# A two-layer streaming encoder on one core: who computes the low halves of the weights beside the recurrence

## The chip, the core and the metric

The kernel runs on one core of a Trainium2 chip. The metric is the device time of one execution in microseconds (us). A core has five engines with a queue of their own, each in program order: TensorE (PE, matmul; PEld is its weight load), VectorE (DVE), ScalarE (ACT), GpSimd (POOL) and SyncE (SP, which here issues all transfers).

## The reference

The reference runs two layers over 1,024 prompt frames and 64 frames of a running stream, each of width 1,024: a layer of RWKV-7 time mixing, a layer of sliding-window attention, and a SwiGLU FFN after each. The first layer matters here.

```python
xr = x + xx * mu[0]            # xx: the previous frame less this one; likewise xk, xv, xw, xa, xg
r = xr @ w_rkv[0]; k = xk @ w_rkv[1]; v = xv @ w_rkv[2]
...
def step(s, inp):              # one frame; s is a 64x64 matrix per head, 16 heads
    r_t, w_t, k_t, v_t, a_t, b_t = inp
    sa = jnp.einsum('bhvk,bhk->bhv', s, a_t)
    s = s * w_t[:, :, None, :] + sa[..., None] * b_t[:, :, None, :] + v_t[..., None] * k_t[:, :, None, :]
    return s, jnp.einsum('bhvk,bhk->bhv', s, r_t)
s_fin, y = lax.scan(step, s0, seq_in)
out = ((groupnorm(y) + bonus) * g) @ w_o
x = x + out
x = x + swiglu(rmsnorm(x, norm_ffn[l]), ffn_w_in[l], ffn_w_out[l])
```

## The kernel before, in words

**Two halves.** The frames are cut into half A (512 prompt frames, chunks 0 to 7 of 64 frames) and half B (512 prompt frames and the 64 of the running stream, chunks 8 to 16). Activations lie with features on the partitions and frames along the free axis.

**Dense products in three matmuls.** `Dense` cuts each operand into a high half (rounded to `fp32r`) and a low half (the remainder), and `mm` adds three products: high by high (L604), low activation by high weight (L605), high activation by low weight (L606). A weight tile of 128x1024 comes in two pieces of 128x512. `piece` loads one (`wr`, L563, by SP), rounds it on ScalarE (`wh`, L564) and subtracts (`wl`, L565). The subtraction runs on GpSimd for every third piece and on VectorE for the other two. There are three buffers for `wr` and six each for `wh` and `wl`. Of half B a dense tile is two groups of 290 columns, so 24 matmuls into one PSUM bank `dp` for each group.

**The recurrence in chunks.** For each chunk `prep` loads r, k, a, s from DRAM and forms scaled operands (GpSimd takes the products of L151, L176, L177), `inverse32` solves a triangular system with a long row of small VectorE steps (L268 and L272 in turn), `chain` runs five groups of matmuls from the old state to the new one (L447 and L448 write the new state, `r_M`), and `post` normalises the chunk's output: L489 on VectorE, L490 and L491 on GpSimd, a transpose on TensorE (L113, into `p_ry`), L496 and L497 on VectorE, and a store to `s_z` (L498). The next chunk's chain needs this chunk's state.

**What runs beside what.** `recur_free(range(8), ...)` issues chunks 0 to 7. Behind it in the code, at a lower priority on TensorE, stand the projections v, r and k of half B (`rkv("B", ...)`, 24 weight tiles, so 48 pieces), their mixes (L850, L851, L597) and the small decay, rate and gate products of half B. A scheduler with a timeline of its own merges all of this into one fixed order for each engine, and each engine then runs its queue in that order. Half A's next step, `mixed_in` and `mix_out` (L1059, L596, L1071), needs `s_z` of all of chunks 0 to 7. Chunks 8 to 16 run later, beside half A's FFN.

Of the kernel before, what the change touches and what calls it, by code (L numbers as in the profile page):

```python
# [12 lines left out]
ALU = mybir.AluOpType  # L13
# [8 lines left out]
def bc(ap, n):  # L22

    return ap.unsqueeze(len(ap.shape)).broadcast_to(list(ap.shape) + [n])
# [7 lines left out]
class Two:  # L32


    def __init__(self, tc):
        self.tc, self.pe = tc, 0
# [48 lines left out]
class Rwkv:  # L85
# [331 lines left out]

    def chain(self, ch, d, M):

        nc = self.nc  # L420
        V, S, G = nc.vector, nc.scalar, nc.gpsimd

        sv = self.t([128, 16, 64], "sv")
        nc.sync.dma_start(sv[64:128].rearrange("p a b -> p (a b)"), self.scr["vt"][ch * 64:ch * 64 + 64, :])
        svh = sv.rearrange("p (j par) v -> p j par v", par=2)
        V.tensor_copy(svh[0:64, :, 0, :], M[0:64])
        S.copy(svh[0:64, :, 1, :], M[64:128])
        E = lambda x: x.rearrange("p (a b) -> p a b", a=8)
        X, W = d["X"], self.W
        heads = [(i, i // 2, slice(64 * (i % 2), 64 * (i % 2) + 64)) for i in range(16)]  # L430
        U0p = E(self.pc())
        for i, j, h in heads:
            self.mm(U0p[h, j, :], lhsT=X[:, 8 * (i % 2) + j, 0:64], rhs=sv[:, i, :], start=True, stop=True)
        U0 = self.tmp()
        S.copy(U0, U0p)
        yield
        Up = E(self.pc())
        for i, j, h in heads:
            self.mm(Up[h, j, :], lhsT=W[h, j, :], rhs=U0[h, j, :], start=True, stop=True)
        V.tensor_copy(svh[0:64, :, 0, :], Up[0:64])  # L440
        S.copy(svh[0:64, :, 1, :], Up[64:128])
        yield
        Sp = E(self.pc())
        for i, j, h in heads:
            self.mm(Sp[h, j, :], lhsT=d["BT"][:, i, :], rhs=sv[:, i, :], start=True, stop=True)
        Mn = d["M"] = self.t([128, 8, 64], "M", 2)
        V.tensor_tensor(out=Mn, in0=Sp, in1=M, op=ALU.add)  # L447
        V.tensor_tensor(out=Mn, in0=Mn, in1=bc(d["PC"], 64), op=ALU.mult)  # L448
        yield


        Y = E(self.p([128, 512], "ry", 1))
        out = lambda j, par: Y[64 * (j % 2):64 * (j % 2) + 64, j // 2 * 2 + par, :]

        def seen(par):
            h = slice(64 * par, 64 * par + 64)
            return [self.mm(out(j, par), lhsT=d["AR"][h, j, 1, :], rhs=M[h, j, :], start=par == 0 and j < 2, stop=False) for j in range(8)]
        even = seen(0)
        by = G.memset(self.t([1, 1], "by", 2), 0.0)
        yield  # L460

        odd = seen(1)
        for i, first in ((by, even[-1]), (odd[0], by)):
            info = mybir.DependencyInfo(mybir.DependencyClass.Sync, mybir.DependencyReason.DATA)
            self.tc.add_manual_dep(i.ins, first.ins.name, info, reason="rows")
        for q in range(0, 8, 2):
            for j, par in ((q, 0), (q + 1, 0), (q, 1), (q + 1, 1)):
                self.mm(out(j, par), lhsT=X[:, 8 * par + j, 64:128], rhs=sv[:, 2 * j + par, :], start=False, stop=q == 6 and par == 1)
        d["Y"] = Y
        yield  # L470
# [51 lines left out]
class Dense:  # L522


    def __init__(self, tc, sb, ps, c):
        self.tc, self.nc, self.sb, self.ps, self.c = tc, tc.nc, sb, ps, c
        self.n = self.turn = 0
        self.more = self.esb = self.pump = None
        self.mixed = []
        self.spare, self.early = deque("x" * RING), deque()  # L530

    def t(self, shape, tag, bufs, dt=F32, sb=None):
# [24 lines left out]
    def piece(self, src, rows=128, raw=None):  # L557
        nc = self.nc
        n = src.shape[1]
        hi, lo = self.t([128, 512], "wh", 6, F32R), self.t([128, 512], "wl", 6, F32R)  # L560
        self.turn += 1
        x, h, l = (raw or self.raw)()[:rows, :n], hi[:rows, :n], lo[:rows, :n]
        nc.sync.dma_start(x, src)  # L563
        nc.scalar.copy(h, x)  # L564
        (nc.gpsimd if self.turn % 3 == 0 else nc.vector).tensor_tensor(out=l, in0=x, in1=h, op=ALU.subtract)  # L565
        return h, l

    @staticmethod
# [177 lines left out]
def tile_stream_step(ctx: ExitStack, tc: tile.TileContext, I, O):  # L746
    nc = tc.nc
# [8 lines left out]
    dn = Dense(tc, sb, ps, c)  # L756
# [42 lines left out]
    def put(name, half, j, stg):  # L799

        c0 = halves[half][2]
        dst = scr[name][c0:c0 + 8, :, j * 64:j * 64 + 64].rearrange("c p t -> p c t")
        nc.sync.dma_start(dst, stg[:, 0:512].rearrange("p (c t) -> p c t", t=64))
        if half == "B":
            nc.sync.dma_start(scr[name][16, :, j * 64:j * 64 + 64], stg[:, SOFF:SOFF + 64])
# [175 lines left out]
    def rkv(half, name, xs, ws=()):  # L981

        T, groups = mixed[half]
        tok0 = halves[half][2] * 64

        def tokens(j, stg):

            p = dn.bank()
            for b in range(4):
                nc.tensor.transpose(p[:, b * 128:b * 128 + 128], stg[:, b * 128:b * 128 + 128], c["id"])  # L990
            vt = dn.st()
            copy_out[half](vt[:, :512], p)
            nc.sync.dma_start(scr["vt"][tok0:tok0 + 512, j * 128:j * 128 + 128].rearrange("(b t) f -> t b f", t=128),
                              vt[:, :512].rearrange("t (b f) -> t b f", f=128))
            if half == "B":
                p = dn.bank()
                nc.tensor.transpose(p[:64, :128], stg[:, SOFF:SOFF + 64], c["id"])
                vt = dn.st()
                copy_out[half](vt[:64, :128], p[:64, :128])
                nc.sync.dma_start(scr["vt"][1024:1088, j * 128:j * 128 + 128], vt[:64, :128])  # L1000

        old = None
        w, early = I["rkv"]["rkv".index(name)], [dn.st() for _ in ws]
        if ws:
            dn.first(ws, xs, groups, lambda j, o, n, p: S.copy(early[j][:, o:o + n], p))
        for j in range(8):
            if j < len(early):
                stg = early[j]
            else:
                stg = dn.st()  # L1010
                dn.full(w[j], xs, groups, lambda o, n, p: copy_out[half](stg[:, o:o + n], p))
            put(name, half, j, stg)
            if name == "v":
                if old:
                    tokens(*old)
                old = (j, stg)
            if j == 7:
                dn.free(*xs)
            yield
        if old:  # L1020
            tokens(*old)
# [3 lines left out]
    def all(gen):  # L1025
        for _ in gen:
            pass
# [138 lines left out]
    def prio(p):  # L1166
        tc.cur_priority = int(p * 1000000)
# [37 lines left out]
    def recur_free(chunks, M, base, low):  # L1205

        def prep(i):
            all(rw.prep(chunks[i], ds[i], wide=True))

        def prep2(i):  # L1210
            rw.inverse32(ds[i])
            rw.turned(ds[i])
        ds = [{} for _ in chunks]
        rw.two.at(base, base)
        prep(0)
        prep2(0)
        for i, ch in enumerate(chunks):
            late = 0.001 * i
            if i + 1 < len(chunks):
                rw.two.at(base + 0.301 + late, low + 0.301 + late)  # L1220
                prep(i + 1)
            rw.two.at(base + late, base + late)
            all(rw.chain(ch, ds[i], M))
            M = ds[i]["M"]
            rw.two.at(base + late, low + late)
            all(rw.post(ch, ds[i]))
            if i + 1 < len(chunks):
                rw.two.at(base + 0.1 + late, base + 0.1 + late)
                prep2(i + 1)
        return M  # L1230
# [78 lines left out]
        step(old, fill)  # L1309

    M = recur_free(range(8), M, 1, LOW)
    prio(2)
    r, k = (mixes("B", hB, n) for n in "rk")
    stage = several(4, chain(deB, raB, gaB))
# [2 lines left out]
    go(rkv("B", "r", xs["Br"]), chain(stage, several(2, take(RING - 8, k))))  # L1317
    all(k)
    all(rkv("B", "k", xs["Bk"]))
    pump = dn.pump = Pump(tc)  # L1320

    def saved(M):
# [79 lines left out]
class Attention:  # L1402
# [170 lines left out]
    def out(self, xs, x, hv, norm):  # L1573
        nc, dn, I = self.nc, self.dn, self.I
        T, groups, _ = hv
        for j in range(8):
            dn.full(I["wo"][j], xs, groups,
                    lambda o_, n, p: nc.vector.scalar_tensor_tensor(
                        out=x[j][:, o_:o_ + n], in0=p, scalar=self.vec["b_o"][:, j:j + 1], in1=x[j][:, o_:o_ + n],
                        op0=ALU.add, op1=ALU.add))  # L1580
            norm.add(x[j][:, :T])
            if j == 7:
                dn.free(*xs)
            yield
# [107 lines left out]
```

## Time and profile before

| | |
|---|---|
| median of three runs | 3019.65 us (3019.26 to 3027.69) |
| the profiled execution: its own time | 3027.17 us |
| its span, first to last instruction | 3025.4 us, 53,491 instructions |
| busy time by engine | PE 2837.6, DVE 1835.6, ACT 1344.4, POOL 916.4 us |
| mean granted TensorE clock | 0.965 of 2.4 GHz |

The profiled execution lies 7.52 us above the median, near the slowest of the three runs. "Busy" counts the time in which an engine had an instruction under way; a VectorE instruction that is held by something else after it was issued counts as busy.

### The profile page before, as it was taken

To read this page: it belongs to the slowest core of one execution; us is meant where nothing else is said; L and a number is where in the kernel's file an instruction comes from. 1 tells how busy PE (TensorE), PEld (TensorE's weight loads), DVE (VectorE), ACT (ScalarE), POOL (GpSimd) and SP (SyncE) were. 2 spreads that over 40 slices of the span, in tenths; PEclk is the share of its full clock that TensorE was granted. 3 is DMA by queue.
4 is the path that set the end of the run, shared out by engine and by line. 5 is a ranking of instruction groups with operands and counts; after the bars stand their busy time and mean duration, and the time that the engine had idled before them with its cause. 6 is when DMAs were issued, how large, how long until landed. Compare 5 with 4: busy or idle time off the path is not lost. (4 is left out here: it accounts for less than half of the span.)

```text
span 3025.4 us, 53491 instructions
## 1 busy us (share of the span) xinstructions
PE 2837.6 (94%) x20802; PEld 2443.9 (81%) x20802; DVE 1835.6 (61%) x3630; ACT 1344.4 (44%) x2485; POOL 916.4 (30%) x795
## 2 busy tenths in 40 slices
PE   6998888887999999999999999999999999999998
PEld 5777777875677777787789999887777888999997
DVE  8887789976778677467553333665644345533334
ACT  6767665543444444244653222344554233322222
POOL 5554124422333333224212222243111222222221
PEclk9999878998999999999999999999999999999999
DMA  4645352345233323432212222222222332322222
GB/s 146 165 123 147 111 155 81 107 113 149 67 92 106 105 84 93 128 118 84 62 50 70 84 84 81 77 84 80 61 69 77 94 94 70 112 83 81 83 84 70
DMA packets 262053, 289.22 MB, mean 96 GB/s; under 512 B 125028, under 2 KB 143972, under 8 KB 261800
## 3 DMA queue, kind: packets, MB, share of 16 engines
q1 hardware_dynamic: 261800, 285.81, 32.0%
q8 instruction: 163, 2.67, 0.4%
q14 instruction: 90, 0.74, 0.1%
HBM read 243.18 MB, written 41.16 MB: 94 GB/s over the span
## 5 line engine op out<-in xcount | busy, mean ns | idle before, releaser
L604 PE MATMUL dp<-xh,wh 128*128 128x288 f32 (+2 forms) x3480 | 1189.6, 343 | 41.6 <-ACT xh L596 15.1
L605 PE MATMUL dp<-xl,wh 128*128 128x288 f32 (+2 forms) x3480 | 1167.8, 336 | 7.5 <-DVE xl L597 5.3
L606 PE MATMUL dp<-xh,wl 128*128 128x288 f32 (+2 forms) x3480 | 1163.1, 334 | 0.0
L564 ACT CAST wh<-wr 128x512 fp32r<-128x512 f32 x730 | 446.9, 619 | 812.8 <-PE dp L605 624.8
L604 PEld LDWEIGHTS dp<-xh,wh 128*128 128x128 f32 x3480 | 664.9, 191 | 124.9 <-ACT xh L596 18.0
L605 PEld LDWEIGHTS dp<-xl,wh 128*128 128x128 f32 x3480 | 665.7, 191 | 69.5 <-DVE xl L597 9.0
L606 PEld LDWEIGHTS dp<-xh,wl 128*128 128x128 f32 x3480 | 665.9, 191 | 56.8 <-issue 2.8
L565 POOL TENSOR_TENSOR wl<-wr,wh 128x512 fp32r<-128x512 f32 x243 | 336.5, 1385 | 1036.2 <-ACT wh L564 944.9
L565 DVE TENSOR_TENSOR wl<-wr,wh 128x512 fp32r<-128x512 f32 x487 | 377.6, 778 | 422.6 <-ACT wh L564 416.4
L604 PE MATMUL dp<-mh,wh 128*128 128x288 f32 (+1 forms) x808 | 254.4, 315 | 4.5 <-DVE hx L1135 2.8
L606 PE MATMUL dp<-mh,wl 128*128 128x288 f32 (+1 forms) x808 | 253.8, 314 | 0.0
L605 PE MATMUL dp<-ml,wh 128*128 128x288 f32 (+1 forms) x808 | 253.7, 314 | 0.0
L1135 DVE TENSOR_TENSOR a_xB<-dp,a_xB 128x288 f32<-128x288 f32 x352 | 158.1, 456 | 85.2 <-PE dp L606 84.8
L1118 POOL TENSOR_TENSOR xl<-st,xh 128x288 fp32r<-128x288 f32 (+1 forms) x102 | 100.6, 986 | 332.3 <-ACT xh L1117 320.0
L1116 DVE TENSOR_TENSOR st<-st,dp 128x288 f32<-128x288 f32 (+1 forms) x132 | 70.1, 531 | 203.7 <-PE dp L606 203.2
L604 PEld LDWEIGHTS dp<-mh,wh 128*128 128x128 f32 x808 | 152.3, 189 | 15.1 <-DVE hx L1135 3.9
L606 PEld LDWEIGHTS dp<-mh,wl 128*128 128x128 f32 x808 | 152.3, 188 | 8.6 <-issue 2.4
L605 PEld LDWEIGHTS dp<-ml,wh 128*128 128x128 f32 x808 | 152.4, 189 | 6.9 <-issue 1.1
L1135 DVE TENSOR_TENSOR hx<-dp,hx 128x512 f32<-128x512 f32 x176 | 119.5, 685 | 42.1 <-PE dp L606 41.2
L1117 ACT CAST xh<-st 128x288 fp32r<-128x288 f32 (+1 forms) x102 | 50.2, 492 | 127.5 <-DVE st L1116 126.4
L1114 ACT ACTIVATE st<-dp 128x288 f32<-128x288 f32 (+1 forms) x132 | 62.2, 471 | 87.5 <-PE dp L606 87.0
L597 POOL TENSOR_TENSOR xl<-st,xh 128x512 fp32r<-128x512 f32 (+2 forms) x37 | 64.7, 1758 | 68.5 <-ACT xh L596 68.5
(378 smaller groups left out, 3851.9 us busy)
## 6 DMA issues: line engine op xcount, KB each, us to landing
wr<-in_ffn_in SPq DMA_DIRECT2D x352, 256.0 KB
wr<-in_ffn_out SPq DMA_DIRECT2D x176, 256.0 KB
wr<-in_rkv SPq DMA_DIRECT2D x90, 256.0 KB
wr<-in_rwo SPq DMA_DIRECT2D x32, 256.0 KB
wr<-in_wq SPq DMA_DIRECT2D x32, 256.0 KB
wr<-in_wo SPq DMA_DIRECT2D x32, 256.0 KB
r_r_s<-s_s SPq DMA_DIRECT2D x17, 256.0 KB
r_sv<-s_vt SPq DMA_DIRECT2D x17, 256.0 KB
```

Source lines behind the costliest of these rows:

```text
L564: nc.scalar.copy(h, x)
L565: (nc.gpsimd if self.turn % 3 == 0 else nc.vector).tensor_tensor(out=l, in0=x, in1=h, op=ALU.subtract)
L597: (eng or self.nc.vector).tensor_tensor(out=lo, in0=x, in1=hi, op=ALU.subtract)
L604: self.nc.tensor.matmul(ps, lhsT=wh, rhs=xh, start=i == 0, stop=False)
L605: self.nc.tensor.matmul(ps, lhsT=wh, rhs=xl, start=False, stop=False)
L606: self.nc.tensor.matmul(ps, lhsT=wl, rhs=xh, start=False, stop=i == last)
L1114: S.activation(t[o], p, AF.Silu)
L1116: V.tensor_tensor(out=t[o], in0=t[o], in1=p, op=ALU.mult)
L1117: S.copy(a.hi[:, q], t[o])
L1118: G.tensor_tensor(out=a.lo[:, q], in0=t[o], in1=a.hi[:, q], op=ALU.subtract)
L1135: V.tensor_tensor(out=self.x[m][:, q], in0=p, in1=self.x[m][:, q], op=ALU.add)
```

## The change: what it does

`Dense` gets a field `share`, which takes the place of the constant 3. It is 3 everywhere but in the code that issues the projections of half B, where it is 1: there every piece's subtraction goes to GpSimd. Of these 48 pieces 16 were on GpSimd before; 32 move from VectorE's queue to GpSimd's. Nothing else is written differently, but the scheduler builds every queue anew.

```diff
@@ class Dense, __init__
         self.mixed = []
+        self.share = 3
         self.spare, self.early = deque("x" * RING), deque()
@@ piece
         nc.scalar.copy(h, x)
-        (nc.gpsimd if self.turn % 3 == 0 else nc.vector).tensor_tensor(out=l, in0=x, in1=h, op=ALU.subtract)
+        (nc.gpsimd if self.turn % self.share == 0 else nc.vector).tensor_tensor(out=l, in0=x, in1=h, op=ALU.subtract)
@@ tile_stream_step
     M = recur_free(range(8), M, 1, LOW)
+
+    dn.share = 1
     prio(2)
     r, k = (mixes("B", hB, n) for n in "rk")
     stage = several(4, chain(deB, raB, gaB))
     go(rkv("B", "v", xs["Bv"]), chain(wait(3), take(8 - 3, stage)))
     all(r)
     go(rkv("B", "r", xs["Br"]), chain(stage, several(2, take(RING - 8, k))))
     all(k)
     all(rkv("B", "k", xs["Bk"]))
+    dn.share = 3
     pump = dn.pump = Pump(tc)
```

Line numbers of the changed kernel are one higher from L530 on, three from L1313 and four from L1323. The queues differ in three places that the prediction speaks of.

**GpSimd in the middle of the recurrence.** The rows are those of the prep of chunk 4 (`r_rt_3763`, `r_rkr_3776`) with the post steps of chunks 1 and 2 beside it (`r_sm_3266`, `r_yc_3269`; `r_sm_3600`, `r_yc_3603`); `wl` are the pieces. Before:

```order
L490 TENSOR_TENSOR r_sm_3266<-r_sm_3266,power 128x8
L565 TENSOR_TENSOR wl_6300<-wr_6301,wh_6299 128x512
L491 TENSOR_TENSOR r_yc_3269<-r_yc_3269,r_sm_3266 128x512
L479 TENSOR_TENSOR r_vf_3493<-r_vf_3493,vecs 128x512
L151 TENSOR_TENSOR r_rt_3763<-r_r_k_3756,vecs 128x8x64
L459 MEMSET r_by_3569 1x1
L156 MEMSET r_rt_3767 128x8
L480 TENSOR_TENSOR r_vf_3159<-r_vf_3159,r_g_3595 128x512
L481 TENSOR_TENSOR r_g_3595<-r_g_3595,vecs 128x512
L176 TENSOR_TENSOR r_rkr_3776<-r_rkr_3776,r_r_r_3755 128x512
L177 TENSOR_TENSOR r_rkr_3776<-r_rkr_3776,vecs 128x512
L565 TENSOR_TENSOR wl_6489<-wr_6490,wh_6488 128x512
```

Of the change, from L481 of `r_g_3595` up to the same piece `wl_6489`:

```order
L481 TENSOR_TENSOR r_g_3595<-r_g_3595,vecs 128x512
L566 TENSOR_TENSOR wl_6294<-wr_6295,wh_6293 128x512
L566 TENSOR_TENSOR wl_6300<-wr_6301,wh_6299 128x512
L151 TENSOR_TENSOR r_rt_3763<-r_r_k_3756,vecs 128x8x64
L156 MEMSET r_rt_3767 128x8
L566 TENSOR_TENSOR wl_6415<-wr_6416,wh_6414 128x512
L176 TENSOR_TENSOR r_rkr_3776<-r_rkr_3776,r_r_r_3755 128x512
L177 TENSOR_TENSOR r_rkr_3776<-r_rkr_3776,vecs 128x512
L566 TENSOR_TENSOR wl_6421<-wr_6422,wh_6420 128x512
L490 TENSOR_TENSOR r_sm_3600<-r_sm_3600,power 128x8
L491 TENSOR_TENSOR r_yc_3603<-r_yc_3603,r_sm_3600 128x512
L566 TENSOR_TENSOR wl_6489<-wr_6490,wh_6488 128x512
```

Between `wl_6300` and `wl_6489` nine steps of the recurrence stood in a row; now two more pieces stand between them, two steps apart, and L151, with which the prep of a chunk begins, stands right behind two pieces.

**The end of chunk 7.** On GpSimd, L490 and L491 of the last chunk of half A (`r_sm_5193`, `r_yc_5196`) and what stands behind them; `wl_7589`, `wl_7636` and `wl_7745` belong to half A's next product, `r_rt_7470` to the prep of chunk 8. Before:

```order
L565 TENSOR_TENSOR wl_7589<-wr_7590,wh_7588 128x512
L481 TENSOR_TENSOR r_g_5188<-r_g_5188,vecs 128x512
L490 TENSOR_TENSOR r_sm_5193<-r_sm_5193,power 128x8
L565 TENSOR_TENSOR wl_7636<-wr_7637,wh_7635 128x512
L491 TENSOR_TENSOR r_yc_5196<-r_yc_5196,r_sm_5193 128x512
L151 TENSOR_TENSOR r_rt_7470<-r_r_k_7463,vecs 128x8x64
L156 MEMSET r_rt_7474 128x8
L151 TENSOR_TENSOR r_rt_7887<-r_r_k_7880,vecs 128x8x64
L176 TENSOR_TENSOR r_rkr_7483<-r_rkr_7483,r_r_r_7462 128x512
```

Of the change:

```order
L490 TENSOR_TENSOR r_sm_5193<-r_sm_5193,power 128x8
L491 TENSOR_TENSOR r_yc_5196<-r_yc_5196,r_sm_5193 128x512
L566 TENSOR_TENSOR wl_7589<-wr_7590,wh_7588 128x512
L566 TENSOR_TENSOR wl_7636<-wr_7637,wh_7635 128x512
L566 TENSOR_TENSOR wl_7745<-wr_7746,wh_7744 128x512
L151 TENSOR_TENSOR r_rt_7470<-r_r_k_7463,vecs 128x8x64
L156 MEMSET r_rt_7474 128x8
L698 TENSOR_TENSOR lo_7586<-lo_7586,st_7626 128x512
L151 TENSOR_TENSOR r_rt_7887<-r_r_k_7880,vecs 128x8x64
L176 TENSOR_TENSOR r_rkr_7483<-r_rkr_7483,r_r_r_7462 128x512
```

The piece between L490 and L491 has gone behind them, and the prep of chunk 8 (L151) stands behind three pieces more. On TensorE, the transpose of chunk 7's output (`p_ry_5153`), the last tiles of B's k projection (`dp_7365`, `dp_7406`, `dp_7432`) and the first of half A's next product (`dp_7560`). Before:

```order
L606 MATMUL dp_7432<-xh_6913,wl_7401 128x290
L604 MATMUL dp_7432<-xh_6920,wh_7400 128x290
L605 MATMUL dp_7432<-xl_6921,wh_7400 128x290
L606 MATMUL dp_7432<-xh_6920,wl_7401 128x290
L113 MATMUL p_ry_5153<-c_id,r_yc_5196 128x128 x4
L604 MATMUL dp_7560<-xh_7494,wh_7548 128x512
L605 MATMUL dp_7560<-xl_7495,wh_7548 128x512
```

Of the change:

```order
L605 MATMUL dp_7365<-xh_6913,wh_7333 128x290
L606 MATMUL dp_7365<-xl_6914,wh_7333 128x290
L113 MATMUL p_ry_5153<-c_id,r_yc_5196 128x128 x4
L607 MATMUL dp_7365<-xh_6913,wl_7334 128x290
L605 MATMUL dp_7365<-xh_6920,wh_7333 128x290
L606 MATMUL dp_7365<-xl_6921,wh_7333 128x290
L607 MATMUL dp_7365<-xh_6920,wl_7334 128x290
L605 MATMUL dp_7406<-xh_6402,wh_7394 128x290
```

Before, all dense matmuls of half B stand ahead of the transpose; now 53 stand behind it. Counted in the order, of the 1,657 dense matmuls (L604 to L606) that stand ahead of `dp_7560`, 1,498 stood ahead of chunk 6's state product (`p_rc` from `r_BT`) before and 1,425 stand there now; up to the same product of chunk 7 another 123 before and 101 now; from there to the transpose 35 before and 78 now.

**The hand-over on SyncE.** The store of chunk 7's output (`s_z`) and what stands around it: `r_r_k` are loads for the preps of chunks 8 and 9, `hx` the loads of half A's next product. Before:

```order
L148 DMA r_r_k_7463<-s_k 128x512
L148 DMA r_r_k_7880<-s_k 128x512
L498 DMA s_z<-r_vf_4829 128x512
L478 DMA r_g_8669<-s_g 128x512
L1059 DMA hx_7492<-s_z 128x8x64
L1059 DMA hx_7499<-s_z 128x8x64
L1059 DMA hx_7506<-s_z 128x8x64
```

Of the change:

```order
L804 DMA s_k<-st_7326 128x8x64
L806 DMA s_k<-st_7326 128x64
L498 DMA s_z<-r_vf_4829 128x512
L564 DMA wr_7692<-in_rwo 128x512
L478 DMA r_g_8669<-s_g 128x512
L1060 DMA hx_7492<-s_z 128x8x64
L1060 DMA hx_7499<-s_z 128x8x64
```

The two loads of `r_r_k`, which wait for the last store of `s_k`, stood ahead of the store of `s_z` and now stand behind the loads of `hx`; L169 of chunk 8, which needs the first of them, has gone behind L497 of chunk 7 on VectorE in the same way.

## Rows read from the trace of the kernel before

**Rows 1.** The page: busy time of two engines; shares of the last chain.

```profile
PE 2837.6 (94%) x20802; PEld 2443.9 (81%) x20802; DVE 1835.6 (61%) x3630; ACT 1344.4 (44%) x2485; POOL 916.4 (30%) x795
PE 34%; DVE 2%; issue 0%; ACT 0%; DMA 0%; SPq 0%; DVEq 0%; ACTq 0%
```

**Rows 2.** Windows: stretch and length (us), busy time by engine (instructions), clock, DMA.

```profile
230.00:390.00 160.00, 140.22 (x1146) 120.96 (x1145) 123.05 (x298) 107.11 (x176) 54.15 (x46) 0.88 0.47 134
390.00:645.00 255.00, 220.68 (x2293) 197.94 (x2292) 233.28 (x622) 149.02 (x235) 92.13 (x71) 0.87 0.39 107
645.00:671.00 26.00, 26.00 (x364) 24.83 (x363) 14.22 (x29) 9.64 (x19) 7.56 (x9) 1.00 0.50 136
671.00:687.00 16.00, 1.53 (x7) 0.97 (x5) 6.28 (x10) 3.95 (x7) 9.29 (x8) 0.61 0.62 160
```

**Rows 3.** Groups by line, 390 to 645 us: busy, mean ns; idle before, releaser.

```profile
L565 DVE TENSOR_TENSOR wl<-wr,wh 128x512 fp32r<-128x512 f32 x21 | 17.3, 825 | 0.0
...
L210 DVE TENSOR_TENSOR r_G<-p_rp,c_mask 128x512 f32<-128x512 f32 x20 | 13.7, 683 | 3.0 <-PE p_rp L109 2.9
...
L248 DVE STREAM_TRANSPOSE r_f<-r_f 128x1024 f32<-128x1024 f32 x5 | 6.2, 1245 | 12.3 <-ACT r_f L243 12.3
```

**Rows 4.** The same view of GpSimd, 390 to 645 us.

```profile
L565 POOL TENSOR_TENSOR wl<-wr,wh 128x512 fp32r<-128x512 f32 x11 | 14.8, 1344 | 50.0 <-ACT wh L564 47.7 <-issue 2.3
```

**Rows 5.** One line's instructions, whole run: duration ns min/median/max.

```profile
L565 DVE TENSOR_TENSOR wl<-wr,wh x487: 647/692/1954, 40.4 to 2988.8; 128x512 fp32r<-128x512 f32 x163
...
L565 POOL TENSOR_TENSOR wl<-wr,wh x243: 1257/1294/3645, 41.0 to 2987.3; 128x512 fp32r<-128x512 f32 x122
```

**Rows 6.** Timeline (start, duration): first and last GpSimd piece, VectorE beside them.

```profile
416.61 1.27 POOL L565 TENSOR_TENSOR wl<-wr,wh 128x512 fp32r<-128x512 f32 x1 [2.16 <-ACT wh L564]
417.87 0.69 DVE L219 TENSOR_TENSOR r_vf<-p_rp,r_vf 128x512 f32<-128x512 f32 x1 [3.10 <-PE p_rp L109]
...
644.54 1.46 POOL L565 TENSOR_TENSOR wl<-wr,wh 128x512 fp32r<-128x512 f32 x1 [10.73 <-ACT wh L564]
644.78 1.25 DVE L484 TENSOR_SCALAR r_sm<-r_sm 128x8 f32<-128x8 f32 x1
```

**Rows 7.** Two VectorE lines over the whole run: duration ns min/median/max.

```profile
L484 DVE TENSOR_SCALAR r_sm<-r_sm x17: 151/171/1252, 357.1 to 1252.9; 128x8 f32<-128x8 f32 x17
...
L497 DVE TENSOR_TENSOR r_vf<-r_g,r_vf x17: 676/691/1780, 373.5 to 1261.2; 128x512 f32<-128x512 f32 x17
```

**Rows 8.** Timeline of the end of chunk 7, several engines, in order of time.

```profile
664.20 0.27 PE L109 MATMUL p_rc<-r_sv,r_BT 128*64 128x64 f32 x1
...
666.22 0.41 PE L605 MATMUL dp<-xl,wh 128*128 128x290 f32 x1
...
666.60 0.29 PE L604 MATMUL dp<-xh,wh 128*128 128x290 f32 x1
...
667.00 0.30 PE L604 MATMUL dp<-xh,wh 128*128 128x290 f32 x1
...
672.56 1.26 POOL L565 TENSOR_TENSOR wl<-wr,wh 128x512 fp32r<-128x512 f32 x1
...
674.88 1.11 PE L113 MATMUL p_ry<-c_id,r_yc 128*128 128x128 f32 x4 [3.72 <-POOL r_yc L491]
...
676.08 0.69 DVE L496 TENSOR_TENSOR r_g<-p_ry,r_g 128x512 f32<-128x512 f32 x1 [5.20 <-issue]
...
677.69 0.69 DVE L169 SCALAR_TENSOR_TENSOR r_rkr<-r_rkr,r_r_k 128x512 f32<-128x512 f32 x1 [0.91 <-DMA r_r_k<-s_k]
...
677.73 1.55 POOL L151 TENSOR_TENSOR r_rt<-r_r_k,vecs 128x512 f32<-128x512 f32 x1 [2.91 <-DMA r_r_k<-s_k]
...
678.30 1.53 DVE L497 TENSOR_TENSOR r_vf<-r_g,r_vf 128x512 f32<-128x512 f32 x1
...
679.86 0.32 SPq L498 DMA_DIRECT2D s_z<-r_vf  x1
...
686.74 0.80 PE L604 MATMUL dp<-xh,wh 128*128 128x512 f32 x1 [10.75 <-ACT xh L596]
```

## The prediction

> **What bounds the kernel now.** I read the page first. The last chain ends almost wholly on TensorE, and VectorE is busy for 61% of the span [rows 1]; over the whole run moving 32 VectorE instructions would be worth nothing. But the change touches only the time in which half B's projections run beside chunks 0 to 7, about 230 to 671 us, so I then read windows. From 390 to 645 us VectorE is busy 233.28 of 255 us and TensorE 220.68, at a clock of 0.87 [rows 2]. The groups by line say what VectorE's idle 21.7 us are: 12.3 wait for ScalarE's copies ahead of L248, 2.9 for TensorE ahead of L210 [rows 3], another 3.1 for TensorE ahead of L219 [rows 6]. So in this stretch VectorE sets the pace of the recurrence. From 645 to 671 us it is the reverse: TensorE is busy all the time, VectorE 14.22 of 26 us. From 671 to 687 us TensorE does next to nothing [rows 2]: it waits 3.72 us for L491 and then, after chunk 7's transposes, 10.75 us for that chunk's output to go to DRAM and come back [rows 8]. Behind this TensorE is near its limit to the end, so the time of the whole kernel moves with the start of half A's next product at 686.74 us.
>
> **The change part by part.** *What leaves VectorE.* In 390 to 645 us it makes 21 pieces, 17.3 us at 825 ns [rows 3]; the other 11 of the 32 lie earlier.
>
> *What comes back as blocking.* A piece takes GpSimd 1294 ns where VectorE needs 692 [rows 5]. And VectorE does not run free beside it. In the first GpSimd piece of the stretch L219, which reads PSUM, takes its usual 0.69 us; in the last, L484 takes 1.25 us [rows 6] where its median is 171 ns [rows 7]. I went through all 11 pieces of rows 4 in this way: 10 lengthen a VectorE instruction, by 10.3 us together, 0.94 us for each of the 11. Most of those held are L268 steps, which have both inputs in SBUF; some are copies. Twenty-one more pieces cost 21 x 0.94 = 19.7 us. The net of the stretch is 19.7 - 17.3 = +2.4 us. Its bounds: nothing is held (L219), -17.3; each piece holds VectorE for its whole 1.29 us, 27.1 - 17.3 = +9.8. I take 0.94 because it is of the same instruction in the same stretch.
>
> The Trainium skill (SBUF — State Buffer, Who interferes with whom) has a rule for this: GpSimd and VectorE share one pair of SBUF ports, an instruction of VectorE with two SBUF inputs or in a two-port mode competes with a GpSimd instruction that reads SBUF, and whoever starts first keeps the pair for its whole instruction. The rows agree on who is held and who is not; if VectorE were always caught at the start, the stretch would be worth +9.8 and the sum below would be 3022.9 us.
>
> *The 11 earlier pieces.* From 230 to 390 us VectorE is busy 123.05 of 160 us [rows 2], so its idle 37 us hide a change of 0.94 - 0.825 = 0.12 us a piece. I cost them at nothing; without that cover they cost 1.3 us.
>
> *TensorE's order.* The scheduler counts VectorE relieved and puts the recurrence earlier against the dense work: 73 dense matmuls fewer ahead of chunk 6's state product. Two L604 starts with two other matmuls between are 667.00 - 666.60 = 0.40 us apart, 0.133 us for each [rows 8], so this is 9.7 us of TensorE. Where VectorE sets the pace most of it is idle time anyway; only what VectorE waits for TensorE can be won, 2.9 + 3.1 = 6.0 us [rows 3, 6]. I take half, -3.0, between 0 and -6.0.
>
> *The end of chunk 7.* From chunk 6's state product to chunk 7's TensorE is full [rows 2], and 101 dense matmuls stand there for 123: 22 x 0.133 = -2.9 us. From there to the transposes took 674.88 - 664.20 = 10.7 us, with the GpSimd piece at 672.56 between L490 and L491 [rows 8]. That piece is gone, but 78 dense matmuls stand there for 35, and with the 2.0 us of chain matmuls ahead of them (664.20 to 666.22) TensorE needs 78 x 0.133 + 2.0 = 12.4: +1.7. After the transposes L496 starts at 676.08 and L497 ends at 679.83; between them lie a wait of 0.91 us and L169, both for chunk 8, and L497 itself is held to 1.53 us by chunk 8's L151 [rows 8]. All of this is moved behind. L497 would end at 676.08 + 0.69 + 0.69 = 677.46: -2.4. The 53 dense matmuls now behind the transposes are 7.1 us and fit in the hole of 10.75 - 2.4 = 8.4 us; if the hole closes further they cost the difference. Together -2.9 + 1.7 - 2.4 = -3.6 us, between -6.0 and, if GpSimd brings L491 late, 0.
>
> *What is late next.* L151, L169 and the loads of chunk 8 start some 10 us later. Three tiles of 24 dense matmuls stand ahead of chunk 8's first matmul in both orders and cover it. `wl_7589`, `wl_7636` are late by the length of two pieces; their tiles come after `hx`, at 686.74 or a little before. Each piece needs its cast, then GpSimd; 48 pieces of 1.3 us are 62 us in more than 400, so GpSimd's throughput is no bound: in the stretch it was busy 92.13 of 255 us [rows 2] and gets 27 more.
>
> **The sum.** +2.4 - 3.0 - 3.6 = -4.2 us. Against the profiled execution's own 3027.17 us that is 3023.0; that execution stands 7.5 us above the median of the three runs, so against the median it is 3019.65 - 4.2 = **3015.5 us**.
>
> **The rivals.** *The blocking is small.* If the new pieces fall on PSUM reads, reductions and transposes as often as not, half of 0.94 us is lost for each: 9.9 - 17.3 = -7.4 in the stretch, with the other terms -14.0, 3005.6 us. For it speaks the first piece of rows 6; against it that only 1 in 11 got off free.
>
> *GpSimd's queue becomes the wait (slower).* A piece waits at the head of GpSimd's queue until ScalarE has cast it: 47.7 us for the 11 pieces [rows 4], 4.3 us each. Nothing behind it moves. Before, nine steps of the recurrence stood between two pieces; now L151 of a prep stands right behind two, and the prep's Square, norm and triangular solve hang on it. If that makes each of the stretch's five solves (L248 x5, rows 3) late by 4.3 us, it is +21.7, by half of that +10.8; in the middle +16.3, and 3015.5 + 16.3 = 3031.8 us. It decides from 13.3 us on, 2.7 us a chunk. Against it speaks that a prep runs about a chunk ahead of its use, and that a piece whose cast is done waits for nothing.
>
> *The change does nothing that counts.* If the pace of the stretch is set by the chain across engines rather than by VectorE's load, and the hole at 671 us only moves, the time stays at 3019.7 us.
>
> The Trainium skill (GPSIMD Engine Reference, Engine selection) advises against two-input elementwise work on GpSimd, at about half of VectorE's rate; 1294 against 692 ns agrees. By that alone the change would be a loss only if GpSimd were full, which it is not.
>
> **How the numbers follow.** A measurement of this kernel can tell about 0.3%, 9 us, from no change. Chances: my sum 0.45, small blocking 0.25, GpSimd's queue 0.20, nothing 0.10. Faster than 3010.6: 0.23 of the second and 0.11 of my own case, whose range is 3007 to 3025 (the stretch 7 us either way, the other terms 3); 0.34. Slower than 3028.7: 0.16 of the third and 0.02 of the first; 0.18. The rest, 0.48, lies within. The range for 8 in 10 runs from 3002, a little beyond the small blocking, to 3031, where the queue's case is half in.
>
> **What would show it.** Right: VectorE still busy some 230 of 255 us in the stretch though 21 instructions poorer, with L268's mean up; L490 and L491 of chunk 7 adjacent; L497 of that chunk about 0.69 us; dense matmuls in the hole behind the transposes; half A's next product some 4 us earlier. Wrong: L248 and L447 of each chunk earlier than before by 2 us more each time (small blocking), or L151 with long idle times behind pieces and VectorE idle ahead of the solves (the queue). What would make the prediction wrong is above all a price of blocking other than 0.94 us, which is read from 11 pieces and multiplied by 21.

## The result, and the profile after

The changed kernel takes 3039.54 us, median of five runs (3038.56 to 3045.52). Five runs of the kernel before, timed beside it, have the median 3027.69 (3019.26 to 3030.08): the three shown above lay low. The ratio is 1.0047, 95% interval 1.0035 to 1.0059, so the change costs some 14 us, 11 to 18 by the interval (ratios are turned into us here by 3027 us; the two medians lie 11.9 us apart). Predicted were -4 us.

The page of the changed kernel: busy time of the engines, and shares of the last chain.

```profile
PE 2851.9 (94%) x20802; PEld 2454.6 (81%) x20802; DVE 1826.9 (60%) x3598; ACT 1342.2 (44%) x2485; POOL 964.4 (32%) x827
PE 34%; DVE 2%; issue 0%; ACT 0%; DMA 0%; SPq 0%; DVEq 0%; ACTq 0%
```

The change did what it says: VectorE is 9 us less busy than in [rows 1], GpSimd 48 us more, and 32 instructions have gone from one to the other. The windows of the changed kernel, columns as in [rows 2]:

```profile
230.00:390.00 160.00, 138.64 (x1079) 119.96 (x1079) 108.01 (x264) 100.08 (x157) 66.10 (x54) 0.81 0.40 118
390.00:645.00 255.00, 213.66 (x2123) 188.60 (x2120) 225.06 (x575) 146.01 (x234) 117.62 (x88) 0.83 0.39 109
645.00:671.00 26.00, 25.00 (x358) 22.92 (x358) 17.95 (x62) 9.88 (x20) 9.79 (x9) 1.00 0.35 100
671.00:687.00 16.00, 16.00 (x177) 15.40 (x176) 5.33 (x10) 5.31 (x11) 5.96 (x7) 1.00 0.44 129
```

TensorE's hole from 671 to 687 us is full (its wait for half A's next product comes later now), and yet fewer of its instructions are done by 645 us (1079 + 2123 against 1146 + 2293), at a lower clock. The groups by line of the same stretch, 390 to 645 us, beside [rows 3] and [rows 4]:

```profile
L268 DVE TENSOR_TENSOR r_f<-r_f,r_f 128x48 f32<-128x48 f32 (+14 forms) x150 | 54.4, 393 | 0.2
...
L566 POOL TENSOR_TENSOR wl<-wr,wh 128x512 fp32r<-128x512 f32 x28 | 42.3, 1512 | 52.9 <-ACT wh L565 52.8
```

and that L268 group in the kernel before:

```profile
L268 DVE TENSOR_TENSOR r_f<-r_f,r_f 128x48 f32<-128x48 f32 (+14 forms) x162 | 49.0, 332 | 0.3
```

One step of the triangular solve takes 393 ns instead of 332, in the mean over 15 shapes. How far the recurrence is behind shows at L448, which writes the new state, of chunks 6 and 7 (count, duration ns, first and last start). Before:

```profile
L448 DVE TENSOR_TENSOR r_M<-r_M,r_PC x2: 691/692/692, 642.2 to 666.2; 128x512 f32<-128x512 f32 x2
```

After:

```profile
L448 DVE TENSOR_TENSOR r_M<-r_M,r_PC x2: 682/688/693, 654.9 to 675.7; 128x512 f32<-128x512 f32 x2
```

Chunk 6 is 12.7 us late, chunk 7 only 9.5: the loss is made before chunk 6's new state, and the end of chunk 7 gives some of it back. That end, in the timeline of the changed kernel (several engines):

```profile
686.73 0.60 PE L113 MATMUL p_ry<-c_id,r_yc 128*128 128x128 f32 x4
...
687.42 0.69 DVE L496 TENSOR_TENSOR r_g<-p_ry,r_g 128x512 f32<-128x512 f32 x1 [5.13 <-PE p_ry L113]
688.15 0.69 DVE L497 TENSOR_TENSOR r_vf<-r_g,r_vf 128x512 f32<-128x512 f32 x1
...
689.85 0.45 SPq L498 DMA_DIRECT2D s_z<-r_vf  x1
...
696.98 0.50 PE L605 MATMUL dp<-xh,wh 128*128 128x512 f32 x1 [2.69 <-ACT xh L597]
```

L497 follows L496 at once and is not held; half A's next product starts at 696.98 instead of 686.74 [rows 8], 10.2 us late, after a wait of 2.69 us instead of 10.75, and the span is 12.0 us longer (3037.4 against 3025.4).

### The profile page after: what moved, and what is told of

Read it like the earlier page. It is cut to its first block, busy times and chain, and to the rows that moved or that the text cites. A ratio compares the mean times of both kernels' runs of the same rounds, so it can differ in the third digit from the quotient of the medians.

```text
span 3037.4 us, 53490 instructions
## 1 busy us (share of the span) xinstructions
PE 2851.9 (94%) x20802; PEld 2454.6 (81%) x20802; DVE 1826.9 (60%) x3598; ACT 1342.2 (44%) x2485; POOL 964.4 (32%) x827
## 5 line engine op out<-in xcount | busy, mean ns | idle before, releaser
L606 PE MATMUL dp<-xl,wh 128*128 128x288 f32 (+2 forms) x3480 | 1171.3, 337 | 15.5 <-POOL xl L598 9.2
L566 POOL TENSOR_TENSOR wl<-wr,wh 128x512 fp32r<-128x512 f32 x275 | 387.5, 1410 | 1102.5 <-ACT wh L565 1012.7
L606 PEld LDWEIGHTS dp<-xl,wh 128*128 128x128 f32 x3480 | 668.2, 192 | 79.1 <-POOL xl L598 11.8
L566 DVE TENSOR_TENSOR wl<-wr,wh 128x512 fp32r<-128x512 f32 x455 | 351.4, 775 | 418.8 <-ACT wh L565 412.7
L606 PE MATMUL dp<-ml,wh 128*128 128x288 f32 (+1 forms) x808 | 253.9, 314 | 0.0
L606 PEld LDWEIGHTS dp<-ml,wh 128*128 128x128 f32 x808 | 152.5, 189 | 6.9 <-issue 1.1
L852 DVE SCALAR_TENSOR_TENSOR es<-hx,vecs,es 128x512 f32<-128x512 f32 (+1 forms) x80 | 82.1, 1062 | 6.2 <-ACT es L851 5.8
```

The costliest lines, as they stand in the source:

```text
L566: (nc.gpsimd if self.turn % self.share == 0 else nc.vector).tensor_tensor(out=l, in0=x, in1=h, op=ALU.subtract)
L606: self.nc.tensor.matmul(ps, lhsT=wh, rhs=xl, start=False, stop=False)
L852: dn.mixed.append(V.scalar_tensor_tensor(out=x, in0=h[:, 0:T], scalar=vec[f"mu{m}"][:, j:j + 1], in1=x, op0=ALU.mult, op1=ALU.add))
```

## The experiments

Two accounts fit this. **A**: the loss is in the new order of the queues. From 230 us to half A's next product TensorE idles no more than before (66.4 against 68.6 us), but loses 60.9 us of its busy time to the lower clock, against 45.3 (a busy microsecond at a granted clock of 0.50 is counted as half lost). **B**: the 32 pieces on GpSimd cost it themselves, either by holding VectorE (**B1**) or by what waits behind them in GpSimd's queue (**B2**).

**Order and engine taken apart.** A first, thrown-away build of the kernel gives the order in which its instructions stand; the real build is then held to that order on every engine. Before's order with the change's engines (shown), and the reverse, in which the two numbers for `share` change places:

```diff
-def tile_stream_step(ctx: ExitStack, tc: tile.TileContext, I, O):
+def tile_stream_step(ctx: ExitStack, tc: tile.TileContext, I, O, share=1, like=None):
...
-    dn.share = 1
+    dn.share = share
...
+def keep_order(tc, like, engines):
...
+    at = {name: k for k, name in enumerate(like)}
+    ours = [i for i in tc.nc.cur_bb.bb.instructions if i.name in at and "PoolBoundary" not in type(i).__name__ and str(i.engine).split(".")[-1] in engines]
+    last = {}
+    for i in sorted(ours, key=lambda i: at[i.name]):
+        if i.engine in last:
+            info = mybir.DependencyInfo(mybir.DependencyClass.NoSync, mybir.DependencyReason.DATA)
+            tc.add_manual_dep(i, last[i.engine], info, reason="like")
+        last[i.engine] = i.name
...
+    with _tile.TileContext(trial, schedule_with_timeline_sim=True) as tc:
+        tile_stream_step(tc, J, Q, share=3)
+    like = [i.name for f in trial.m.functions for b in f.blocks for i in b.instructions]
     with _tile.TileContext(nc, schedule_with_timeline_sim=True) as tc:
         tile_stream_step(tc, I, O)
+        keep_order(tc, like, ('PE', 'DVE', 'Activation', 'Pool', 'SP'))
```

> Every queue keeps the order of the kernel before; only the 32 subtractions stand on GpSimd, at the places where the scheduler had let them go on VectorE. Theory A (the loss comes from the new order of the queues, in which TensorE spends more of its busy time at the lower clock: 60.9 us of clock lost between 230 us and half A's next product against 45.3 before): the clock loss goes back to about 45 us and the time is within 5 us of before or below it, 3010 to 3030 us on the scale of before. Theory B (the 32 GpSimd pieces cost it themselves, by holding VectorE or by waiting at the head of GpSimd's queue): about the time of the change, 10 to 15 us above before.

> Every queue keeps the order of the changed kernel, but 32 of the 48 subtractions go back to VectorE, to the places where the scheduler had let them go on GpSimd. Theory A (order): about the time of the change, 8 to 16 us above before, with the long stretch of lower clock near 350 us still there. Theory B (the pieces on GpSimd): within 4 us of before. If VectorE's load counts by itself, this one is even slower than the change, by up to the 26 us that VectorE had less of.

Measured: before's order with the pieces on GpSimd 1.0026 (1.0014 to 1.0037), +8 us. That lies between the 5 us of A and the 10 to 15 of B and decides nothing by itself; but TensorE's lost clock is back at 45.7 us, as A had it, and the time is not. The change's order with the pieces back on VectorE 1.0000 (0.9987 to 1.0013), where A had 8 to 16 us, although 52.4 us of clock are lost in it. So with the engines held, this order is worth nothing that can be measured; with the order held, the pieces cost 8 us in one order and 14 in the other. For this change A falls. Its stretch of low clock is there all the same: 30 us of each trace at 0.50, which is 1.2 GHz, in the changed kernel

```profile
352.00:382.00 30.00, 29.95 (x245) 25.82 (x246) 15.81 (x36) 14.01 (x22) 7.76 (x6) 0.50 0.28 78
```

and in the same order with the pieces on VectorE

```profile
345.00:375.00 30.00, 29.98 (x245) 25.82 (x246) 15.39 (x37) 13.99 (x22) 6.47 (x5) 0.50 0.29 78
```

The second is as fast as before with it.

In two kernels with the same order each VectorE instruction has a partner, and the trace says where the one falls behind the other. The timeline of a solve shows both sides of the trade. The kernel before:

```profile
634.20 0.38 DVE L268 TENSOR_TENSOR r_f<-r_f,r_f 128x88 f32<-128x88 f32 x2
634.50 0.48 DVE L272 TENSOR_REDUCE r_f<-r_f 128x44 f32<-128x132 f32 x2
634.90 0.36 DVE L268 TENSOR_TENSOR r_f<-r_f,r_f 128x80 f32<-128x80 f32 x2
635.19 0.45 DVE L272 TENSOR_REDUCE r_f<-r_f 128x40 f32<-128x120 f32 x2
635.56 0.68 DVE L565 TENSOR_TENSOR wl<-wr,wh 128x512 fp32r<-128x512 f32 x1
636.15 0.36 DVE L268 TENSOR_TENSOR r_f<-r_f,r_f 128x72 f32<-128x72 f32 x2
```

The same steps with before's order and the pieces on GpSimd:

```profile
638.35 1.49 DVE L268 TENSOR_TENSOR r_f<-r_f,r_f 128x88 f32<-128x88 f32 x2
...
638.40 1.35 POOL L566 TENSOR_TENSOR wl<-wr,wh 128x512 fp32r<-128x512 f32 x1 [3.77 <-ACT wh L565]
...
639.76 0.48 DVE L272 TENSOR_REDUCE r_f<-r_f 128x44 f32<-128x132 f32 x2
...
640.04 1.28 POOL L566 TENSOR_TENSOR wl<-wr,wh 128x512 fp32r<-128x512 f32 x1 [0.29 <-ACT wh L565]
...
640.17 1.38 DVE L268 TENSOR_TENSOR r_f<-r_f,r_f 128x80 f32<-128x80 f32 x2
641.47 0.44 DVE L272 TENSOR_REDUCE r_f<-r_f 128x40 f32<-128x120 f32 x2
641.84 0.34 DVE L268 TENSOR_TENSOR r_f<-r_f,r_f 128x72 f32<-128x72 f32 x2
```

Two steps are held by 1.1 and 1.0 us. The piece that is gone had a duration of 0.68 us, but the next step started 0.59 us after it: its last 0.09 us lay under that step. Its removal saves 0.59 us. The Trainium skill (Perfetto Trace Analysis, Optimizing Scalar/DVE Operations) says that part of a profiled VectorE duration overlaps with the next instruction, and that work moved between VectorE and GpSimd may not help, since they share a port. The trace agrees: the overlap is 0.09 us here, and this move costs 8 us.

Summed over the VectorE instructions from the first to the last partner in 390 to 645 us (of the first kernel). The time from one start to the next is divided into the instruction's own part and the idle time behind it; the table has the changes, in us:

| first and second kernel | own part of the pieces gone | own part of all others | idle time | sum |
|---|---|---|---|---|
| before; its order, pieces on GpSimd | 21: -15.8 | +19.2 | +4.1 | +7.5 |
| change's order, pieces on VectorE; the change | 20: -16.1 | +22.7 | +2.5 | +9.1 |

Most of the pieces gone had an own part of 0.60 us; three of the 21 and five of the 20 had been held themselves and had 1.15 to 1.88. None of the added idle time is put down to GpSimd.

**None on GpSimd, and another third.** `dn.share = 1000000` for the whole of half B's projections; and 16 pieces on GpSimd as before, but others:

```diff
-    dn.share = 1
+    dn.turn += 1
...
-    dn.share = 3
+    dn.turn -= 1
```

> The opposite edit: all 48 subtractions of half B's projections on VectorE, none on GpSimd, the queues built anew by the scheduler. Theory B (a GpSimd piece costs more than the VectorE piece it replaces): some 5 us faster than before, half of the change's loss with the other sign, since 16 pieces move instead of 32. Theory A (order): no fixed sign, anywhere within 15 us of before.

> As before, 16 of the 48 subtractions on GpSimd, but each is the piece ahead of the one of before: the same load on every engine, the queues built anew. Theory B: within 3 us of before. Theory A: the time moves by more than its noise though no load moved, 5 to 15 us either way, together with TensorE's lost clock.

Measured: none on GpSimd 0.9952 (0.9935 to 0.9969), 14.5 us faster than before; another third 1.0006 (0.9993 to 1.0019), no change. So 0, 16 and 48 pieces stand at -14.5, 0 to 2 and +14 us, as if a GpSimd piece cost more than the VectorE piece that it replaces. B expected 5 us for the first step and it is three times that, still within the 15 us either way that A allowed. The queues of these kernels differ in order too, and another order can count by itself (10 us in a case below), so these two runs do not part the pieces from the order.

**Held, or queued?** In the order of the kernel with none on GpSimd, each piece gets an extra GpSimd instruction that waits for the same cast: two fills with zeros, or the subtraction itself into a scrap buffer. VectorE makes all 48 in both.

```diff
-        nc.scalar.copy(h, x)
+        cast = nc.scalar.copy(h, x)
...
+        if self.extra == "fill":
+            for _ in range(2):
+                e = nc.gpsimd.memset(self.scrap, 0.0)
+                self.behind(e, cast)
...
+        if self.extra == "subtract":
+            e = nc.gpsimd.tensor_tensor(out=self.scrap[:rows, :n], in0=x, in1=h, op=ALU.subtract)
```

> All 48 subtractions on VectorE, in the order that the kernel with all of them on VectorE has on every engine; beside each, GpSimd fills a scrap buffer twice with zeros (some 1.2 us), and waits for the same cast as a piece would. The fills read nothing. Theory B1 (a GpSimd instruction that reads SBUF holds VectorE): within 3 us of the kernel with all 48 on VectorE, 14 us below before. Theory B2 (the wait at the head of GpSimd's queue and GpSimd's time delay the recurrence): about as slow as with real pieces there, 14 to 25 us above that kernel, so at or above before.

> The same, but the extra GpSimd instruction beside each piece is the subtraction itself (128x512, two inputs from SBUF, 1.3 us), written to the scrap buffer; VectorE still makes all 48. Theory B1 (held): 48 pieces at 0.6 to 0.94 us with nothing taken off VectorE, 20 to 40 us above the kernel with all 48 on VectorE, 6 to 26 us above before. Theory B2 (queue): the same as with the fills.

Measured: fills 0.9963 (0.9948 to 0.9978), subtractions 1.0081 (1.0064 to 1.0098): 3 and 39 us above the kernel with none (each with 7 us either way), as B1 had it. Groups by line, 390 to 645 us: with none

```profile
L268 DVE TENSOR_TENSOR r_f<-r_f,r_f 128x48 f32<-128x48 f32 (+14 forms) x145 | 35.5, 272 | 0.3
```

with the fills

```profile
L268 DVE TENSOR_TENSOR r_f<-r_f,r_f 128x48 f32<-128x48 f32 (+14 forms) x155 | 36.4, 262 | 0.3
...
L571 POOL MEMSET lo<- 128x584 f32 x64 | 38.2, 596 | 72.2 <-ACT wh L565 70.6
```

with the subtractions

```profile
L268 DVE TENSOR_TENSOR r_f<-r_f,r_f 128x48 f32<-128x48 f32 (+14 forms) x140 | 44.6, 346 | 0.2
...
L575 POOL TENSOR_TENSOR lo<-wr,wh 128x512 f32<-128x512 f32 x30 | 60.1, 2003 | 63.0 <-issue 32.4 <-ACT wh L565 30.2
```

The fills wait as long for the casts as the pieces of any kernel here, and L268 does not feel them; beside the subtractions it goes from 272 to 346 ns. By partners, the 32 extra subtractions of this stretch make it 27.0 us longer: 28.1 us of longer instructions, 0.88 for each, and 1.2 us less idle time. The 64 fills make it 3.0 us longer. An extra subtraction also keeps `wr` and `wh` in use for longer, which a fill does not; as VectorE's idle time did not grow, that is not the cause here. In this stretch B1 is shown and B2 is not needed. From 230 to 390 us it is the same: 16 extra subtractions put the kernel 18.6 us behind, 12.7 of it longer instructions, and the fills at the same places 3.6 us. The subtractions also run longer than a piece had to in [rows 5], so GpSimd is held too. The Trainium skill (SBUF — State Buffer, Who interferes with whom) has it that an instruction of VectorE with two SBUF inputs competes with a GpSimd instruction that reads SBUF, not with one that only writes; both runs agree.

**Which pieces.** The projections apart, first in orders made for them. The edit of v alone is shown; in the other two runs the three numbers are 1000000, 1000000, 1 (k alone) and 1000000, 1, 1 (r and k):

```diff
-    dn.share = 1
     prio(2)
...
+    dn.share = 1
     go(rkv("B", "v", xs["Bv"]), chain(wait(3), take(8 - 3, stage)))
     all(r)
+    dn.share = 1000000
     go(rkv("B", "r", xs["Br"]), chain(stage, several(2, take(RING - 8, k))))
     all(k)
+    dn.share = 1000000
     all(rkv("B", "k", xs["Bk"]))
```

> GpSimd makes the 16 remainders of projection v alone, VectorE those of r and k; the queues built anew. Most of v's pieces lie ahead of 390 us, where VectorE has idle time. If a GpSimd piece costs only where VectorE is busy without a break, as the prediction's step on the 11 earlier pieces says, the time is within 4 us of the kernel with all 48 on VectorE, 14 us below before. If every GpSimd piece costs the same wherever it lies (0.85 us for each, from the 13.5 us between 0 and 16 pieces), it is at the time of before.

> GpSimd makes the 16 remainders of projection k alone, which lie between about 500 and 645 us, where VectorE has no idle time; VectorE makes those of v and r. If the cost is that of a held VectorE in the full stretch, 16 pieces cost 16 x (0.94 - 0.60) to 16 x 0.94 us, 5 to 15 us above the kernel with all 48 on VectorE: 9 us below before to the time of before. If only the order matters, no fixed sign.

> The change without its early part: GpSimd makes the 32 remainders of r and k, VectorE the 16 of v; the queues built anew. The change stands 28.8 us above the kernel with all 48 on VectorE, v alone 19.1, k alone 10.9 (ratios x 3027). If r costs as much as k, this one is 22 us above it, 7 above before. If the costs of the three add up to the change's, r costs nothing and it is 10 us above it, 4 below before.

Measured: v alone 1.0015 (1.0006 to 1.0024), k alone 0.9988 (0.9978 to 0.9998), r and k 1.0024 (1.0013 to 1.0034). Above the kernel with none on GpSimd that is 19, 11 and 22 us, and the change 29. v's early pieces are not free: 19 us is even more than with the same price everywhere. k's 11 lie within the 5 to 15 expected, and r and k stand at the 22 expected if r costs as much as k. The three parts do not add up to the change. For v the order was held again:

> GpSimd makes the 16 remainders of projection v, and every queue keeps the order of the kernel that has all 48 on VectorE. If v's 19.6 us come from its pieces (held VectorE, and GpSimd's queue ahead of the start of the recurrence): 15 to 20 us above that kernel again. If they come from the order that the scheduler made for them: within 6 us of it.

> All 48 subtractions on VectorE, and every queue keeps the order of the kernel that has v's 16 on GpSimd. If v's 19.6 us come from its pieces: within 4 us of the kernel with all 48 on VectorE in its own order. If they come from the order: 15 to 20 us above it.

Measured: v's pieces in the order of none 0.9974 (0.9963 to 0.9986), none in the order of v 0.9984 (0.9972 to 0.9997): 7 and 10 us above the kernel with none, and 19 with both. Neither reading held alone. v's pieces cost 7 us in an order not made for them and 9 (0.9984 to 1.0015) in their own, and that order costs 10 by itself (each with 5 to 6 us either way, so that the 7 is barely clear of nothing).

What early pieces do is seen in the change's order, where two things meet ahead of 390 us. VectorE and GpSimd from 251 to 266 us, with the pieces on VectorE:

```profile
251.53 1.79 POOL L566 TENSOR_TENSOR wl<-wr,wh 128x512 fp32r<-128x512 f32 x1
...
254.58 0.82 DVE L678 TENSOR_TENSOR xl<-ls,xl 32x290 fp32r<-32x290 f32 x2
255.43 1.56 DVE L852 SCALAR_TENSOR_TENSOR es<-hx,vecs,es 128x580 f32<-128x580 f32 x2
...
257.05 3.30 POOL L598 TENSOR_TENSOR xl<-es,xh 128x580 fp32r<-128x580 f32 x2 [3.72 <-ACT xh L597]
...
260.38 0.86 DVE L130 TENSOR_REDUCE lanes<-c_id 128x1 f32<-128x64 f32 x6 [1.34 <-POOL xl L598]
```

and in the changed kernel:

```profile
252.47 5.16 POOL L598 TENSOR_TENSOR xl<-es,xh 128x580 fp32r<-128x580 f32 x3
253.16 3.18 DVE L678 TENSOR_TENSOR xl<-ls,xl 32x290 fp32r<-32x290 f32 x2
256.37 3.65 DVE L852 SCALAR_TENSOR_TENSOR es<-hx,vecs,es 128x580 f32<-128x580 f32 x2
...
257.58 3.56 POOL L566 TENSOR_TENSOR wl<-wr,wh 128x512 fp32r<-128x512 f32 x2
261.10 1.40 POOL L598 TENSOR_TENSOR xl<-es,xh 128x580 fp32r<-128x580 f32 x1
262.46 1.28 POOL L566 TENSOR_TENSOR wl<-wr,wh 128x512 fp32r<-128x512 f32 x1
263.70 1.41 POOL L598 TENSOR_TENSOR xl<-es,xh 128x580 fp32r<-128x580 f32 x1
...
265.14 0.85 DVE L130 TENSOR_REDUCE lanes<-c_id 128x1 f32<-128x64 f32 x6 [5.13 <-POOL xl L598]
```

L678 and L852 are held beside L598 and the pieces, and of GpSimd's queue two pieces have come ahead of the last two remainders of v's mix (L598), and a third between them. L130 waits for the last: the recurrence's first instruction on VectorE starts 4.8 us late. By partners the change falls 6.6 us behind between 230 and 390 us, and so do v's 16 pieces in the order of none (6.6). How much of that is the queue and how much the holding, no run tells apart in these orders; the extra subtractions and fills above say that holding can do it.

**A faster version.** None of the 48 on GpSimd, and the remainders of the mixes r and k on VectorE too:

```diff
-            xs.append(dn.split(x, eng=G if j % (2 if T == TA else 4) else V, late=late))
+            xs.append(dn.split(x, eng=G if j % (2 if T == TA else 4) and not (T != TA and m in (0, 2)) else V, late=late))
```

> All 48 subtractions on VectorE, and also the 12 remainders of half B's mixes r and k (128x580, of 16 in all) that GpSimd made beside the recurrence; the queues built anew. By the held time that they cost before (12.8 us for 12 between 390 and 645 us) against some 0.7 us each on VectorE: 2 to 5 us faster than the kernel with all 48 on VectorE. If they cost VectorE as much as they held it: the same time.

Measured: 0.9944 (0.9931 to 0.9956), 17 us faster than before. Against 0.9952 without the mixes the intervals overlap, so whether the mixes add to it stays open.

## Why the prediction was wrong

- **What bounds the stretch** was right: VectorE is still busy 225 of 255 us, near the 230 forecast.
- **The net of the stretch failed**: +2.4 us was forecast, and with the order held it is +7.5 and +9.1, within the stated bounds of -17.3 and +9.8. *What leaves VectorE* was priced at 21 x 0.825 = 17.3 us by busy time, and the pieces gone had own parts of 15.8 and 16.1. A piece of 0.69 us that is not held gives back 0.60, and the mean of 825 ns held three pieces that were themselves held; at 0.60 each only 12.6 and 12.0 us leave. Whether such a hold leaves with the piece or falls on a later instruction, no run tells apart. *Blocking* was forecast at 19.7 us; the other instructions grew by 19.2 and 22.7. *VectorE's idle time* was given no growth, and grew by 4.1 and 2.5 us; why, stays open.
- **One reading behind the bounds was wrong.** L219 of [rows 6] was taken as an instruction that is not held. It starts at 417.87 us, when the GpSimd piece ends, after 3.10 us in which VectorE was idle: that piece met no VectorE instruction at all. The other 10 of the 11 each held one, by 1.03 us on average. So these rows spoke for no case without a hold, and the rival of small blocking lost its only support.
- **The 11 earlier pieces failed too**: they were put at nothing, hidden by 37 us of idle time in 230 to 390 us. In the change's order they cost 6.6 us, in before's order about 1. The 37 us are spread over 160, and near the start of the recurrence there are hardly any: before, VectorE is busy 9.9 of the 10 us from 250 to 260 (columns as in [rows 2]):

```profile
250.00:260.00 10.00, 9.55 (x60) 8.59 (x59) 9.88 (x10) 6.14 (x13) 5.83 (x4) 1.00 0.51 129
```

- **The end of chunk 7** was right in its parts. From L448 of chunk 6 to that of chunk 7 24.0 became 20.8 us (-3.2; -2.9 forecast); from there to the transposes 8.7 became 11.0 (+2.3; +1.7); from these to the end of L497 5.0 became 2.1 (-2.8; -2.4). Not forecast were +1.2 us from there to the next product: the store of `s_z` is issued 1.0 us after L497's end, behind stores of `s_k` in SyncE's queue. Together -2.5 for -3.6.
- **TensorE's order**, -3.0, can't be told from nothing. It and the end of chunk 7 belong to the order alone, together -6.6. In the profiled execution of the change's order with the pieces on VectorE half A's next product starts 4.3 us earlier than before (682.39 for 686.74), but the times of 12 runs give 1.0000, with 4 us either way:

```profile
682.39 0.79 PE L605 MATMUL dp<-xh,wh 128*128 128x512 f32 x1 [3.25 <-ACT xh L597]
```

- **The sum.** Measured against that kernel the change falls 6.6 us behind from 230 to 390 us and 9.1 more by 645 us, and is 14.6 us late at half A's next product (696.98); the ratios give 14. So what the order does came out at -4 to 0 us for -6.6, and what the engine does at +14 for +2.4: that is where the forecast failed.
- **The rivals.** Small blocking is refuted. GpSimd's queue had the right sign and, with 3031.8 us, a time not far off, but by luck: in the stretch none of the added idle time is put down to GpSimd, and fills that wait as long for the casts cost 3 us in all. Where a queue may have counted is ahead of L130, which the prediction did not look at.

## What to carry to other kernels

Beside a VectorE that is full of instructions with two inputs in SBUF, GpSimd is not free capacity: each 128x512 subtraction there, two inputs read from SBUF, made VectorE's instructions 0.9 to 1.1 us longer, more than the 0.6 us of doing it on VectorE. Price an instruction that leaves an engine by the distance from its start to the next start, not by its duration, and price held ones apart. Idle time hides a cost only where it lies, so look at it in short windows. Where a scheduler builds the queues anew, hold the order and change the engine alone, and the reverse, before reading anything out of the new trace.

## What had not been expected

TensorE ran 30 us at 1.2 GHz without a gap to speak of (busy 29.98 of 30.00) in a kernel that is as fast as before, and TensorE's lost clock, 15.6 us more in the changed kernel, looked like the whole loss until the same stretch turned up there. The time is not a straight line in the number of pieces: from 0 to 16 of them it grows by 14.5 us, with the next 32 by about 14. As the order changes along with them, why is not shown.
